# A decoder layer on one core: sums, first evictions, loads and three steps put in another order

## The chip, the cores and the metric

The kernel runs on one core of a Trainium2 chip. The metric is device time in microseconds (us) of one execution; a kernel's time is the median of its runs. Engines: TensorE (PE) multiplies matrices into PSUM; ScalarE (ACT) and VectorE (DVE) read PSUM and SBUF and write SBUF; GpSimd (POOL) does small work on SBUF; SyncE (SP) issues transfers (DMA). Each engine works through its own queue in order, and semaphores hold one engine until another has finished something.

## What is computed

One layer with two token mixers side by side, for 256 tokens of width 1024, all in float32:

```python
n = rms_norm(h, norm1_g)
proj = n @ w_in            # moba q,k,v | gla q,k,v, gate-down, out-gate | branch gates
mq = rms_norm(mq per head); mk = rms_norm(mk per head)          # 8 heads of 64
y_moba = softmax(mq @ mk.T * 64**-0.5 + t5_bias, causal) @ mv
log_a = log_sigmoid(g_low @ gla_gate_up + gla_gate_bias) / 16
y_gla = rms_norm(gla(gq, gk, gv, log_a), gla_out_norm_g) * silu(g_out)   # 4 heads, dk 128, dv 256
mixed = sigmoid(gate_moba) * (y_moba @ w_branch_moba) + sigmoid(gate_gla) * (y_gla @ w_branch_gla)
h = h + mixed @ w_out
h = h + relu(rms_norm(h, norm2_g) @ w_up)**2 @ w_down
```

With 256 tokens there is one MoBA block, so MoBA is plain causal attention with a bias by distance.

## The kernel before

**Precision in halves.** Every float32 operand of a large matmul is used as a high part in float32r and a low part, x - high. Weights come from HBM into `raw` tiles of 128 x 2048 (1 MB, a *unit* of half the depth and 512 columns, numbered 0 to the end); `split` (line 87) has ACT write the high part `wh` (L94, two pieces of 1024), and `rest` (line 97) has DVE write the low part `wl` (L98, two pieces), one slot later through `defer` and `flush`. There are four `raw` tiles; when the second low piece of unit i is written, `rest` issues the load of unit i + 4 on SP (`load`, line 79, L85).

**The projection.** The loop at line 749 runs over 13 column groups (`IN_ORDER`), each of two units, and each unit over two token tiles: a *slot* is one unit and one token tile, slot number 2 * unit + tile. `block` (line 114) multiplies a plain unit, 12 matmuls of 512 columns a slot; `block_t` (line 122) a transposed one (GQ and GK, GLA's q and k), 8 of 512 and 8 of 256. Behind the block a slot runs `flush`, then `split` of the unit two further on, then the eviction of a finished group, and then the steps that `at(slot, ...)` has put there. This order in the text is the order in every engine's queue.

**The start.** Units 0 and 1 (MQ, MoBA's q) come with x in `xw` tiles and are multiplied by `first_block` while they arrive. The evictions of MQ and MK need `rstd`, one over the root mean square of each token: `x_stats` sums the squares of the x tiles `xs` on ACT (L237), DVE and POOL finish it (L218, L219). So MQ and MK are evicted late, at slots 5 to 8: `m_evac` copies (L301) and squares (L303) on ACT, and DVE and POOL make the heads' norms.

**The steps that are touched.** `split_bias`, `make_bias`, `spread_bias` and `load_bias` make the table of biases: a small matmul, a copy u to SBUF, u to DRAM (`ud`, 12 KB), spread there to 128 rows (`ur`, 1.5 MB), and read back skewed into `bias` (1 MB); all three transfers stand in SP's queue. `g_diag` and `g_row` turn `rstd` into a row (matmul `prow`), which GLA's q and k need. `m_norm` and `m_transpose` norm q and k of MoBA and transpose them into `mqH`, `mqL`, `mkH`, `mkL` (high on ACT L287, low on DVE L288). `m_scores0` (line 336, matmuls L334) multiplies the first 128 tokens and DVE scales and adds the bias (L345); `m_max`, `m_softmax`, `m_weights` follow, and `m_scores1` twice for the other tokens. g_evac (line 536) evicts a transposed slot: a copy `half` on ACT (L542) and two instructions on DVE (L545, L546). `m_evac` of MV writes `mvH` on ACT (L287) and `mvL` on DVE (L288).

Of the kernel before, what the change touches and what calls it, by code (L numbers as in the profile page):

```python
# [22 lines left out]
H = 8  # L23
# [12 lines left out]
MQ, MK, MV, GQ, GK, GV0, GV1 = 0, 512, 1024, 1536, 2048, 2560, 3072  # L36
GLOW = 3584
GO0, GO1, GA0, GA1, GG0, GG1 = 3600, 4112, 4624, 5136, 5648, 6160
TRANSPOSED = (GQ, GK)
IN_ORDER = (MQ, MK, GQ, GK, MV, GV0, GV1, GO0, GO1, GA0, GG0, GA1, GG1)  # L40


V_G2, V_GB, V_OG, V_QG, V_KG, NVEC = 0, 8, 12, 14, 15, 16
# [3 lines left out]
def block_kernel(ctx, tc, xw0_d, xw_d, x_d, vec_d, w_d, up_d, bias_d, out_d):  # L47
    nc = tc.nc
    P = 128
# [14 lines left out]
    def mid(name):  # L64
        return t2.tile([P, 512], F32, name=name, tag="t2")
# [4 lines left out]
    def mmbank(name):  # L70
        return ps.tile([P, 512], F32, name=name, tag="mm")

    def axbank(name):
        return ps.tile([P, 512], F32, name=name, tag="ax")
# [4 lines left out]
    def load(i, pieces=1):  # L79
        if i >= NHU:  # L80
            return
        raw[i] = wp.tile([P, 4, 512], F32, name=f"raw{i}", tag="raw", bufs=4)
        n = 4 // pieces
        for a in range(0, 4, n):
            nc.sync.dma_start(raw[i][:, a:a + n, :], w_d[i - 2, :, a:a + n, :])  # L85

    def split(i, a, n=2):
        if i >= NHU:
            return
        if a == 0:  # L90
            wH[i] = wp.tile([P, 4, 512], F32R, name=f"wh{i}", tag="wh")
            wL[i] = wp.tile([P, 4, 512], F32R, name=f"wl{i}", tag="wl")
        s = slice(a, a + n)
        nc.scalar.activation(wH[i][:, s, :], raw[i][:, s, :], AF.Copy)  # L94
        defer(rest, i, s)
# [10 lines left out]
    def defer(f, *a):  # L106
        deferred.append((f, a))

    def flush():
        now, deferred[:] = list(deferred), []  # L110
        for f, a in now:
            f(*a)
# [26 lines left out]
    vec = const.tile([P, NVEC + 128], F32, name="vec")  # L139
# [10 lines left out]
        nc.sync.dma_start(xw[kt], xw_d[kt - 1])  # L150
    load(2, 2)
    load(3)
    nc.sync.dma_start(vec, vec_d)

    NBR = bias_d.shape[0]
    smallR, smallS = big("smallR"), big("smallS", F32R)
# [66 lines left out]
    xs = [big(f"xs{t}") for t in range(NT)]  # L223
    for t in range(NT):
        nc.sync.dma_start(xs[t], x_d[:, t, :])
    nc.sync.dma_start(biasR, bias_d)
    nc.sync.dma_start(gup, up_d)
    load(4)
    load(5)

    rstd = const.tile([P, NT], F32, name="rstd")
# [14 lines left out]
    T = {}  # L246
# [15 lines left out]
    bias = t4.tile([P, H, 256], F32, name="bias", tag="t8", bufs=3)  # L262
# [5 lines left out]
    def make_bias():  # L268
        pb = axbank("pbias")
        nc.tensor.matmul(pb[:H, :384], biasS[:, :H], biasS[:, H:], start=True, stop=True)  # L270
        u = mid("u")[:H, :384]
        nc.vector.tensor_copy(u, pb[:H, :384])
        T["ud"] = dr.tile([H, 384], F32, name="ud")
        nc.sync.dma_start(T["ud"], u)

    def spread_bias():

        T["ur"] = dr.tile([P, H, 384], F32, name="ur")
        nc.sync.dma_start(T["ur"], T["ud"][None].to_broadcast([P, H, 384]))

    def load_bias():
        ur = T["ur"]
        nc.sync.dma_start(bias, bass.AP(tensor=ur.tensor, offset=ur.offset + 127,
                                        ap=[[H * 384 - 1, P], [384, H], [1, 256]]))

    def split_evac(dH, dL, src, scale):
# [5 lines left out]
    def m_evac(which, t, acc):  # L292
        if which == "mv":
            if t == 0:
                T["mvH"], T["mvL"] = (big(f"mv{a}", F32R).rearrange("p (t c) -> p t c", t=2) for a in "HL")
            split_evac(T["mvH"][:, t, :], T["mvL"][:, t, :], acc, rstd[:, t:t + 1])
            return
        if t == 0:
            T[which] = big(which)
        dst = T[which].rearrange("p (t c) -> p t c", t=2)[:, t, :]  # L300
        nc.scalar.activation(dst, acc, AF.Copy, scale=rstd[:, t:t + 1])  # L301
        sq = mid("sq")
        nc.scalar.activation(sq, acc, AF.Square, scale=rstd[:, t:t + 1])  # L303
        r = T[which, "r", t] = small("rsm", H)

        def finish():
            ss = small("ssm", H)
            nc.vector.tensor_reduce(ss, sq.rearrange("p (h d) -> p h d", d=DH), axis=AX.X, op=OP.add)
            rsqrt(r, ss, DH)

        defer(finish)
# [224 lines left out]
    def g_evac(which, h, acc):  # L536

        if h == 0:
            T[which] = big(which)
        v = T[which][:, h * S:(h + 1) * S]  # L540
        half = mid("half")[:, :S]
        nc.scalar.activation(half, acc[:, S:], AF.Copy)  # L542

        def finish():
            nc.vector.tensor_tensor(v, acc[:, :S], half, op=OP.add)  # L545
            nc.vector.scalar_tensor_tensor(v, v, DK ** -0.5 if which == "gq" else 1.0, rrow,  # L546
                                           op0=OP.mult, op1=OP.mult)

        defer(finish)
# [96 lines left out]
    def silu_evac(g, t, acc):  # L646
        if t == 0:
            T["silu", g] = big(f"silu{g}").rearrange("p (t c) -> p t c", t=2)
        sg = mid("sg")
        nc.scalar.activation(sg, acc, AF.Sigmoid, scale=rstd[:, t:t + 1])  # L650
        nc.vector.scalar_tensor_tensor(T["silu", g][:, t, :], acc, rstd[:, t:t + 1], sg,
                                       op0=OP.mult, op1=OP.mult)
# [6 lines left out]
    def gv_evac(g, t, acc):  # L659
        if t == 0:  # L660
            for a in "HL":
                T["gv" + a, g] = big(f"gv{a}{g}", F32R).rearrange("p (t c) -> p t c", t=2)
        split_evac(T["gvH", g][:, t, :], T["gvL", g][:, t, :], acc, rstd[:, t:t + 1])

    evac = {
        MQ: lambda t, a: m_evac("mq", t, a), MK: lambda t, a: m_evac("mk", t, a),
        MV: lambda t, a: m_evac("mv", t, a),
        GQ: lambda t, a: g_evac("gq", t, a), GK: lambda t, a: g_evac("gk", t, a),
        GV0: lambda t, a: gv_evac(0, t, a), GV1: lambda t, a: gv_evac(1, t, a),
        GO0: lambda t, a: silu_evac(0, t, a), GO1: lambda t, a: silu_evac(1, t, a),  # L670
        GA0: lambda t, a: gate_evac("A", 0, t, a), GA1: lambda t, a: gate_evac("A", 1, t, a),
        GG0: lambda t, a: gate_evac("G", 0, t, a), GG1: lambda t, a: gate_evac("G", 1, t, a),
    }


    steps = {}

    def at(slot, f, *a):
        steps.setdefault(slot, []).append((f, a))

    at(5, split_bias)
    at(8, make_bias)
    at(4, x_stats)
    at(6, g_diag)
    at(7, low_split)
    at(8, g_row)
    at(9, gup_split)
    at(9, m_norm, "mq", 0)
    at(10, m_norm, "mq", 1)
    at(10, spread_bias)  # L690
    at(11, m_norm, "mk", 0)
    at(11, g_low)
    at(12, m_norm, "mk", 1)
    at(13, m_transpose, "mq", 0)
    at(13, m_transpose, "mq", 1)
    at(14, g_decay, 0)
    at(14, g_decay, 1)
    at(14, load_bias)
    at(15, m_transpose, "mk", 0)
    at(15, m_transpose, "mk", 1)  # L700
    at(16, m_scores0)
    at(16, m_max, 0)
    at(17, m_softmax, 0, 0, 4)
    at(18, m_softmax, 0, 4, 8)
    at(19, m_scores1, 0)
    at(19, m_max, 1)
    at(19, m_weights, 0)
    at(20, m_softmax, 1, 0, 2)
    at(21, m_softmax, 1, 2, 4)
    at(22, m_scores1, 1)  # L710
    at(22, m_max, 2)
    at(22, m_weights, 1)
    at(23, m_softmax, 2, 0, 2)
    at(24, m_softmax, 2, 2, 4)
    at(25, g_logsig)
    at(26, g_scan)
    at(26, m_weights, 2)
    at(27, g_exp, "eb")
    at(28, g_exp, "einv")
    at(29, g_exp, "edec")  # L720
# [24 lines left out]
    at(50, g_yT, 1, 1)  # L745


    hu = 0
    for u, col in enumerate(IN_ORDER):
        acc = [] if col in TRANSPOSED else [(axbank if u == 1 else mmbank)(f"acc{t}") for t in range(NT)]  # L750
        for g in range(2):
            if u == 0:
                for k in range(4):
                    first_block(4 * g + k, acc)
            for t in range(NT):
                if col in TRANSPOSED:
                    acc = mmbank("acct")
                    for k in range(2):
                        block_t(hu, t, k, xHL[k], acc)
                elif u:  # L760
                    block(hu, t, xH[g], xL[g], acc[t], g == 0, g == 1)
                flush()
                split(hu + 2, 2 * t)
                if g == 1 and u < 2:
                    at(5 + 2 * u + t, evac[col], t, acc[t])
                elif col in TRANSPOSED:
                    evac[col](2 * g + t, acc)
                elif g == 1:
                    evac[col](t, acc[t])
                for f, a in steps.pop(2 * hu + t, []):  # L770
                    f(*a)
            hu += 1
    assert not steps


    mxH = [kview(big(f"mxH{g}", F32R)) for g in range(2)]
# [58 lines left out]
    for n in range(2):  # L835
        acc = [mmbank(f"po{t}") for t in range(NT)]
# [77 lines left out]
    acc = [axbank(f"pu{j}") for j in range(4)]  # L914
# [15 lines left out]
    for c in range(1, NC):  # L930
        for b in range(2):
            for j in range(2):
                acc = axbank(f"pu{j}")
# [86 lines left out]
```

## Time and profile before

| | us |
|---|---|
| median of 3 runs (424.61 to 425.13) | 424.98 |
| the profiled execution | 424.48 |
| its span, first to last instruction | 422.8 |
| PE busy | 412.9 (98%) |
| weight loads into PE busy | 345.5 (82%) |
| DVE busy | 285.9 (68%) |
| ACT busy | 222.5 (53%) |
| mean granted clock of PE | 0.991 |

The profile is of one execution. Busy time of PE counts matmuls whose ends are modelled, so PE is busy nearly all the time and what matters is where it is not, and where its clock is granted at half (the page's line PEclk shows one slice of 40 at 6 tenths, near 63 to 74 us, and 9 or more in all others). The DMA engines are busy 50% of the span on SP's queue, and nearly all of the time from 5 to 30 us.

### The profile page before, as it was taken

The numbers are of one execution on the slowest core, as the hardware profiler recorded it, in microseconds if no ns is written. First come the engines' busy times: TensorE is split into PE (matmuls) and PEld (weight loads), VectorE is DVE, ScalarE is ACT, GpSimd is POOL, SyncE is SP. The second block draws the span as 40 slices with busy tenths as digits, with TensorE's granted clock in tenths as the row PEclk, the third lists the DMA queues.
The fourth block names the chain that finished last, engine by engine and source line by source line (L and its number), as shares of the span: only waits on it lengthen the run. The fifth ranks groups of instructions, "written<-read, shape, count | busy, mean of one in ns | idle before, by whom it ended". The sixth has DMA issues, their size and how long they took to land.

```text
span 422.8 us, 5266 instructions
## 1 busy us (share of the span) xinstructions
PE 412.9 (98%) x2072; PEld 345.5 (82%) x2072; DVE 285.9 (68%) x374; ACT 222.5 (53%) x344; POOL 17.8 (4%) x21
## 2 busy tenths in 40 slices
PE   8999979999999999999999999999999999999996
PEld 5877957888888888888888888888888888888885
DVE  5838987688798543874856878848393848474753
ACT  5669562869865464553423446646362726263520
POOL 2006100000002011000000000000000000000000
PEclk9999996999999999999999999999999999999999
DMA  8995783245544252372675445645455463627002
GB/s 281 381 372 203 258 289 122 87 189 200 198 164 156 86 194 99 135 279 84 219 279 188 136 174 198 228 172 212 186 184 214 147 250 112 287 101 298 0 2 99
DMA packets 13848, 78.91 MB, mean 187 GB/s; under 512 B 1448, under 2 KB 3104, under 8 KB 5376
## 3 DMA queue, kind: packets, MB, share of 16 engines
q1 hardware_dynamic: 13392, 77.28, 50.0%
q10 hardware_dynamic: 432, 1.31, 0.9%
q8 instruction: 16, 0.26, 0.2%
q14 instruction: 8, 0.07, 0.0%
HBM read 77.52 MB, written 2.63 MB: 190 GB/s over the span
## 4 chain that ended last, share of the span: by engine, by line
PE 84%; DMA 5%; DVE 5%; ACT 4%; issue 1%; SPq 0%; ACTq 0%
PE pu L131 14%; PE acc L118 8%; PE acc L119 8%; PE acc L120 8%; PE pu L133 7%; PE fa L119 7%; PE fa L120 7%; PE fa L118 7%; DMA raw<-w 4%; PE po L118 2%; PE po L120 2%; PE pg L118 2%; PE po L119 2%; PE pg L120 2%; PE pg L119 2%; DVE wl L98 2%
## 5 line engine op out<-in xcount | busy, mean ns | idle before, releaser
L98 DVE TENSOR_TENSOR wl<-raw,wh 128x1024 fp32r<-128x1024 f32 x132 | 158.2, 1220 | 18.9 <-ACT wh L94 18.7
L94 ACT ACTIVATE wh<-raw 128x1024 fp32r<-128x1024 f32 x132 | 135.2, 1051 | 24.4 <-PE pg L120 9.8
L131 PE MATMUL pu<-hHL,wh 128*128 128x512 f32 x256 | 69.9, 394 | 0.0
L118 PE MATMUL acc<-wh,xHL 128*128 128x512 f32 x160 | 64.6, 404 | 0.0
L119 PE MATMUL acc<-wl,xHL 128*128 128x512 f32 x160 | 63.0, 394 | 0.0
L120 PE MATMUL acc<-wh,xHL 128*128 128x512 f32 x160 | 62.9, 393 | 0.0
L131 PEld LDWEIGHTS pu<-hHL,wh 128*128 128x128 f32 x256 | 44.3, 189 | 6.3
L120 PE MATMUL fa<-wh,fL 128*128 128x512 f32 x124 | 48.4, 390 | 0.0
L119 PE MATMUL fa<-wl,fH 128*128 128x512 f32 x124 | 48.4, 390 | 0.0
L118 PE MATMUL fa<-wh,fH 128*128 128x512 f32 x124 | 48.3, 389 | 0.0
L133 PEld LDWEIGHTS pu<-hHL,wl 128*128 128x128 f32 x256 | 39.3, 189 | 5.4
L133 PE MATMUL pu<-hHL,wl 128*128 128x256 f32 x256 | 40.7, 281 | 0.0
L870 ACT ACTIVATE half<-pu 128x256 f32<-128x256 f32 x32 | 12.0, 377 | 54.4 <-PE pu L133 54.4
L871 DVE TENSOR_TENSOR sq<-pu,half 128x256 f32<-128x256 f32 x32 | 13.5, 423 | 34.9 <-ACT half L870 34.2
L120 PEld LDWEIGHTS acc<-wh,xHL 128*128 128x128 f32 x160 | 30.4, 190 | 6.7
L118 PEld LDWEIGHTS acc<-wh,xHL 128*128 128x128 f32 x160 | 30.5, 190 | 6.3
L119 PEld LDWEIGHTS acc<-wl,xHL 128*128 128x128 f32 x160 | 30.6, 191 | 5.7
L120 PEld LDWEIGHTS fa<-wh,fL 128*128 128x128 f32 x124 | 23.3, 188 | 4.9
L118 PEld LDWEIGHTS fa<-wh,fH 128*128 128x128 f32 x124 | 23.3, 188 | 4.7
L119 PEld LDWEIGHTS fa<-wl,fH 128*128 128x128 f32 x124 | 23.3, 188 | 4.7
L876 ACT ACTIVATE fH<-sq 128x512 fp32r<-128x512 f32 x16 | 10.1, 632 | 20.6 <-DVE sq L873 20.6
L131 PE MATMUL acct<-xHL,wh 128*128 128x512 f32 x64 | 17.6, 396 | 0.0
(232 smaller groups left out, 533.8 us busy)
## 6 DMA issues: line engine op xcount, KB each, us to landing
raw<-w SPq DMA_DIRECT2D x65, 1024.0 KB, 4.8
xw<-xw SPq DMA_DIRECT2D x7, 384.0 KB, 6.5
ur<-ud SPq DMA_DIRECT2D x1, 1536.0 KB, 9.2
raw<-w SPq DMA_DIRECT2D x2, 512.0 KB, 7.3
xs<-xs SPq DMA_DIRECT2D x2, 512.0 KB, 8.7
bias<-ur SPq DMA_DIRECT2D x1, 1024.0 KB, 7.4
xr<-xs ACTq DMA_DIRECT2D x2, 512.0 KB, 4.8
out<-o SPq DMA_DIRECT2D x3, 256.0 KB, 2.0
```

The lines of the kernel that those rows point to most:

```text
L94: nc.scalar.activation(wH[i][:, s, :], raw[i][:, s, :], AF.Copy)
L98: nc.vector.tensor_tensor(wL[i][:, s, :], raw[i][:, s, :], wH[i][:, s, :].bitcast(F32), op=OP.subtract)
L118: nc.tensor.matmul(acc, aH[:, k, tk], h, start=start and k == 0, stop=False)
L119: nc.tensor.matmul(acc, aH[:, k, tk], low, start=False, stop=False)
L120: nc.tensor.matmul(acc, aL[:, k, tk], h, start=False, stop=stop and k == 3)
L131: nc.tensor.matmul(acc, tile_(wH, k), a[:, k, :], start=g == 0 and k == 0, stop=False)
L133: nc.tensor.matmul(acc[:, :S], tile_(wL, k), a[:, k, :S], start=False, stop=g == 1 and k == 3)
L870: nc.scalar.activation(half, acc[:, S:], AF.Copy)
L871: nc.vector.tensor_tensor(o, acc[:, :S], half, op=OP.add)
L876: nc.scalar.activation(H, v, AF.Copy)
```

## The change

`IN_ORDER` has MV third, so GQ and GK come a place later (and the weights are laid out in that order). `vec` is loaded behind unit 4 and no longer ahead of x; unit 4 is loaded behind x and ahead of `vec`, `biasR` and `gup`. `ud`, `ur` and `bias` are issued by POOL (`nc.gpsimd`) and no longer by SP. `x_stats` stands at slot 3 and no longer 4. The evictions of MQ and MK stand between `flush` and `split` of slots 4, 5 and 7, 8, where they stood behind `split` of slots 5 to 8. `split_bias` goes from slot 5 to 7, `low_split` from 7 to 8, `make_bias` from 8 to 9, `load_bias` from 14 to 12. `m_scores0` and all that follows of MoBA's softmax go one slot back.

```diff
-IN_ORDER = (MQ, MK, GQ, GK, MV, GV0, GV1, GO0, GO1, GA0, GG0, GA1, GG1)
+IN_ORDER = (MQ, MK, MV, GQ, GK, GV0, GV1, GO0, GO1, GA0, GG0, GA1, GG1)
...
     load(3)
-    nc.sync.dma_start(vec, vec_d)
...
         nc.sync.dma_start(xs[t], x_d[:, t, :])
+    load(4)
+    nc.sync.dma_start(vec, vec_d)
     nc.sync.dma_start(biasR, bias_d)
     nc.sync.dma_start(gup, up_d)
-    load(4)
     load(5)
...
-        nc.sync.dma_start(T["ud"], u)
+        nc.gpsimd.dma_start(T["ud"], u)
...
-    at(5, split_bias)
-    at(8, make_bias)
-    at(4, x_stats)
+    at(3, x_stats)
...
-    at(16, m_scores0)
-    at(16, m_max, 0)
+    at(17, m_scores0)
+    at(17, m_max, 0)
...
                 flush()
+                for f, a in early.pop(2 * hu + t, []):
+                    f(*a)
                 split(hu + 2, 2 * t)
                 if g == 1 and u < 2:
-                    at(5 + 2 * u + t, evac[col], t, acc[t])
+                    early.setdefault(4 + 3 * u + t, []).append((evac[col], (t, acc[t])))
```

ACT's queue behind the splits of unit 3, before; in these rows wh_260 is unit 4, wh_312 unit 5, acc_180 and acc_181 the two token tiles of MQ, xs the x tiles:

```order
L94 ACTIVATE wh_260<-raw_172 128x1024
L237 ACTIVATE junk,ssx<-xs_166 128x1024
L237 ACTIVATE junk,ssx<-xs_167 128x1024
L94 ACTIVATE wh_260<-raw_172 128x1024
L265 ACTIVATE smallS<-smallR 112x392
L301 ACTIVATE mq<-acc_180,rstd 128x512
L303 ACTIVATE sq<-acc_180,rstd 128x512
L94 ACTIVATE wh_312<-raw_174 128x1024
L469 ACTIVATE diag<-diagf 128x256
```

and now, where unit 4 is wh_273 and unit 5 wh_319:

```order
L237 ACTIVATE junk,ssx<-xs_165 128x1024
L237 ACTIVATE junk,ssx<-xs_166 128x1024
L301 ACTIVATE mq<-acc_180,rstd 128x512
L303 ACTIVATE sq<-acc_180,rstd 128x512
L94 ACTIVATE wh_273<-raw_169 128x1024
L301 ACTIVATE mq<-acc_181,rstd 128x512
L303 ACTIVATE sq<-acc_181,rstd 128x512
L94 ACTIVATE wh_273<-raw_169 128x1024
L94 ACTIVATE wh_319<-raw_174 128x1024
```

The sums of x stand ahead of all of unit 4's split, and each of MQ's two evictions ahead of a half of it.

DVE's queue around MoBA's first scores, before; wl_599 is unit 9, wl_679 unit 10, gk and gq the evictions of GLA's k and q, s the scaled scores:

```order
L509 TENSOR_SCALAR gm<-pz,vec 128x256 x4
L98 TENSOR_TENSOR wl_599<-raw_374,wh_598 128x1024
L545 TENSOR_TENSOR gk<-acct,half 128x256
L546 SCALAR_TENSOR_TENSOR gk<-gk,rrow 128x256
L98 TENSOR_TENSOR wl_599<-raw_374,wh_598 128x1024
L545 TENSOR_TENSOR gk<-acct,half 128x256
L546 SCALAR_TENSOR_TENSOR gk<-gk,rrow 128x256
L288 SCALAR_TENSOR_TENSOR mkL<-pt,vec,mkH 128x4x128 x2
L345 SCALAR_TENSOR_TENSOR s_681<-ps_682,bias 128x4x128
L345 SCALAR_TENSOR_TENSOR s_681<-ps_683,bias 128x4x128
L370 TENSOR_REDUCE nmax<-s_681 128x8
L98 TENSOR_TENSOR wl_679<-raw_450,wh_678 128x1024 x2
```

and now, where wl_571 is unit 9 and wl_653 unit 10:

```order
L546 SCALAR_TENSOR_TENSOR gq<-gq,rrow 128x256
L98 TENSOR_TENSOR wl_571<-raw_369,wh_570 128x1024
L545 TENSOR_TENSOR gq<-acct,half 128x256
L546 SCALAR_TENSOR_TENSOR gq<-gq,rrow 128x256
L288 SCALAR_TENSOR_TENSOR mkL<-pt,vec,mkH 128x4x128 x2
L98 TENSOR_TENSOR wl_653<-raw_430,wh_652 128x1024
L545 TENSOR_TENSOR gk<-acct,half 128x256
L546 SCALAR_TENSOR_TENSOR gk<-gk,rrow 128x256
L345 SCALAR_TENSOR_TENSOR s_681<-ps_682,bias 128x4x128
L345 SCALAR_TENSOR_TENSOR s_681<-ps_683,bias 128x4x128
L370 TENSOR_REDUCE nmax<-s_681 128x8
L98 TENSOR_TENSOR wl_653<-raw_430,wh_652 128x1024
```

The evictions ahead of `mkL` are those of q and no longer of k (v's two low halves stand further up), a low half of unit 10 and one of k's evictions have come between `mkL` and the scaled scores, and the other half of unit 10 is behind them.

POOL's queue behind the start, before:

```order
L219 TENSOR_TENSOR rstd<-rsv,mhalf 128x2
L219 TENSOR_TENSOR rsm<-rsv,mhalf 128x8 x4
L563 COPY gx<-eb 128x4x64
L568 COPY gx<-edec 128x4x64
L570 MEMSET at_1261 128x1024
```

and now:

```order
L218 TENSOR_TENSOR rstd<-rsv,mhalf 128x2
L218 TENSOR_TENSOR rsm<-rsv,mhalf 128x8 x4
L274 DMA ud<-u 8x384
L279 DMA ur<-ud 128x3072
L283 DMA bias<-ur 128x8x256
L563 COPY gx<-eb 128x4x64
L568 COPY gx<-edec 128x4x64
```

The three transfers stand between the powers and GLA's copies; on SP they are gone from between the loads.

## Rows read from the trace of the kernel before

**Rows 1.** Who PE waited for, from the table of waits: total us, times, longest.

```profile
PE ps L334 <- DVE mkL L288: 2.9, 1, 2.9
...
PE prow L478 <- ACT diag L469: 0.7, 1, 0.7
PE ps L334 <- ACT mkH L287: 0.7, 1, 0.7
PE acct L133 <- DVE wl L98: 0.6, 1, 0.6
```

**Rows 2.** Busy table: start:end, length, busy of five engines, PEclk, DMA share, GB/s.

```profile
20.00:25.00 5.00, 5.00 (x23) 4.14 (x23) 1.00 (x1) 0.00 (x0) 0.00 (x0) 1.00 1.03 353
...
30.00:35.00 5.00, 3.56 (x18) 2.38 (x17) 4.45 (x10) 4.44 (x9) 1.64 (x1) 1.00 0.74 280
...
80.00:422.80 342.80, 339.37 (x1709) 286.63 (x1707) 229.74 (x282) 173.08 (x252) 6.45 (x5) 1.00 0.46 169
...
64.00:65.00 1.00, 0.60 (x6) 0.61 (x8) 1.00 (x2) 0.00 (x0) 0.00 (x0) 0.50 0.75 180
...
70.00:71.00 1.00, 1.00 (x5) 0.83 (x4) 1.00 (x2) 1.00 (x7) 0.00 (x0) 0.77 0.00 0
```

**Rows 3.** PE's timeline, 27 to 75 us: start, us, instruction, count, idle before it.

```profile
27.75 1.07 PE L131 MATMUL acct<-xHL,wh 128*128 128x512 f32 x4
...
33.38 1.09 PE L131 MATMUL acct<-xHL,wh 128*128 128x512 f32 x4
...
41.77 0.27 PE L488 MATMUL plow<-xHL,lowS 128*96 128x256 f32 x1
...
43.65 1.08 PE L131 MATMUL acct<-xHL,wh 128*128 128x512 f32 x4
...
64.39 0.47 PE L334 MATMUL ps<-mkL,mqH 64*128 64x128 f32 x1 [2.92 <-DVE mkL L288]
...
67.15 0.79 PE L118 MATMUL acc<-wh,xHL 128*128 128x512 f32 x1
...
71.53 0.40 PE L118 MATMUL acc<-wh,xHL 128*128 128x512 f32 x1
...
74.26 0.39 PE L118 MATMUL acc<-wh,xHL 128*128 128x512 f32 x1
```

**Rows 4.** ACT's timeline, 25 to 30 us.

```profile
25.06 1.06 ACT L94 ACTIVATE wh<-raw 128x1024 fp32r<-128x1024 f32 x1 [5.50 <-DMA raw<-w]
26.02 1.05 ACT L237 ACTIVATE junk<-xs 128x1024 f32<-128x1024 f32 x1
...
29.48 0.67 ACT L301 ACTIVATE mq<-acc,rstd 128x512 f32<-128x512 f32 x1
```

**Rows 5.** DVE's timeline, 29 to 84 us.

```profile
29.60 0.16 DVE L266 TENSOR_TENSOR smallS<-smallR,smallS 48x8 fp32r<-48x8 f32 x1 [1.20 <-ACT smallS L265]
29.78 1.23 DVE L98 TENSOR_TENSOR wl<-raw,wh 128x1024 fp32r<-128x1024 f32 x1
...
33.02 1.22 DVE L98 TENSOR_TENSOR wl<-raw,wh 128x1024 fp32r<-128x1024 f32 x1
...
52.86 0.42 DVE L545 TENSOR_TENSOR gk<-acct,half 128x256 f32<-128x256 f32 x1
...
63.60 1.40 DVE L288 SCALAR_TENSOR_TENSOR mkL<-pt,vec,mkH 128x512 fp32r<-128x512 f32 x2
67.03 1.29 DVE L345 SCALAR_TENSOR_TENSOR s<-ps,bias 128x512 f32<-128x512 f32 x2 [2.04 <-PE ps L334]
...
69.50 2.35 DVE L98 TENSOR_TENSOR wl<-raw,wh 128x1024 fp32r<-128x1024 f32 x2
...
83.04 0.75 DVE L288 SCALAR_TENSOR_TENSOR mvL<-acc,rstd,mvH 128x512 fp32r<-128x512 f32 x1
```

**Rows 6.** The page's DMA issues: KB each, median us from issue to landing.

```profile
ur<-ud SPq DMA_DIRECT2D x1, 1536.0 KB, 9.2
...
bias<-ur SPq DMA_DIRECT2D x1, 1024.0 KB, 7.4
```

More of the change, by code (lines that the diff above doesn't have):

```diff
@@ L273, in make_bias @@
         T["ud"] = dr.tile([H, 384], F32, name="ud")
-        nc.sync.dma_start(T["ud"], u)
+        nc.gpsimd.dma_start(T["ud"], u)
     def spread_bias():
         T["ur"] = dr.tile([P, H, 384], F32, name="ur")
-        nc.sync.dma_start(T["ur"], T["ud"][None].to_broadcast([P, H, 384]))
+        nc.gpsimd.dma_start(T["ur"], T["ud"][None].to_broadcast([P, H, 384]))
     def load_bias():
         ur = T["ur"]
-        nc.sync.dma_start(bias, bass.AP(tensor=ur.tensor, offset=ur.offset + 127,
+        nc.gpsimd.dma_start(bias, bass.AP(tensor=ur.tensor, offset=ur.offset + 127,
                                         ap=[[H * 384 - 1, P], [384, H], [1, 256]]))
@@ L679, in at @@
         steps.setdefault(slot, []).append((f, a))
-    at(5, split_bias)
-    at(8, make_bias)
-    at(4, x_stats)
+    at(3, x_stats)
     at(6, g_diag)
-    at(7, low_split)
     at(8, g_row)
+    at(7, split_bias)
+    at(8, low_split)
     at(9, gup_split)
+    at(9, make_bias)
     at(9, m_norm, "mq", 0)
@@ L693, in block_kernel @@
     at(12, m_norm, "mk", 1)
+    at(12, load_bias)
     at(13, m_transpose, "mq", 0)
@@ L697, in block_kernel @@
     at(14, g_decay, 1)
-    at(14, load_bias)
     at(15, m_transpose, "mk", 0)
     at(15, m_transpose, "mk", 1)
-    at(16, m_scores0)
-    at(16, m_max, 0)
[L703 to L714, printed above, removed]
+    at(17, m_scores0)
+    at(17, m_max, 0)
+    at(18, m_softmax, 0, 0, 4)
+    at(19, m_softmax, 0, 4, 8)
+    at(20, m_scores1, 0)
+    at(20, m_max, 1)
+    at(20, m_weights, 0)
+    at(21, m_softmax, 1, 0, 2)
+    at(22, m_softmax, 1, 2, 4)
+    at(23, m_scores1, 1)
+    at(23, m_max, 2)
+    at(23, m_weights, 1)
+    at(24, m_softmax, 2, 0, 2)
+    at(25, m_softmax, 2, 2, 4)
     at(25, g_logsig)
     at(26, g_scan)
-    at(26, m_weights, 2)
+    at(27, m_weights, 2)
     at(27, g_exp, "eb")
@@ L745, in block_kernel @@
     at(50, g_yT, 1, 1)
-    hu = 0
+    hu, early = 0, {}
     for u, col in enumerate(IN_ORDER):
@@ L772, in block_kernel @@
             hu += 1
-    assert not steps
+    assert not steps and not early
     mxH = [kview(big(f"mxH{g}", F32R)) for g in range(2)]
```

## The prediction

> **What bounds the kernel now.** I read four views, in this order. First what TensorE (PE) waited for: after the start it has four waits, 2.9, 0.7, 0.7 and 0.6 us [rows 1]. Three belong to the first stretch (weights' low half, the diagonal for `prow`), the largest to the first score matmuls, which stood until the low half of the normed and transposed k (`mkL`) was written. Second, the busy table by stretch [rows 2]: from 80 us on PE is busy 339.37 of 342.80 us at a granted clock of 1.00, so nothing is to be had there; all that the change can win lies before 72 us. The same table shows the clock: it stays 1.00 (2.4 GHz) in 30 to 35 us, where PE was busy only 3.56 of 5, but it is 0.50 (1.2 GHz) from 64 us, after the long wait, until it comes back inside 70 to 71 (0.77).
>
> Third, PE's own timeline [rows 3], to price stalls and slow clock in one number. PE starts unit 4 at 27.75 and has done the scores and both of the next slots' blocks at 71.53: 43.78 us. The undisturbed work in it: a slot of a transposed unit lasts (41.77 - 33.38) / 3 = 2.80, a plain one 74.26 - 71.53 = 2.73, `g_low` 43.65 - 41.77 = 1.88, the 24 score matmuls half of 67.15 - 64.39 = 1.4 at full clock, and the small ones (bias, `prow`, 16 transposes, decay) an estimate of 2.5 from their starts in the same timeline. Eight transposed and two plain slots: 22.4 + 5.5 + 1.9 + 1.4 + 2.5 = 33.7. So PE lost 10.1 us here. The other way of counting, waits of 4.9 plus 0.17 for each of the four (a matmul's row lasts 0.40 but the next starts 0.23 after it, so a wait reads that much short) plus half of the 6 us at half clock, gives 8.6. I take 10.1 as what there is, and 8.6 as the lower end. Fourth, ACT and DVE in front of that wait: both are backed up from 25 to 64 us, after ACT had stood 5.5 us for the weights of unit 4 [rows 4].
>
> **Part 1: x's sums and the evictions of q ahead of the splits, loads reordered.** The x tiles landed long before they were used: unit 4's weights landed at 25.06 [rows 4], and behind x in the queue lay 1.05 MB of these and 0.37 MB of bias and gate tables; at the 353 GB/s of the stretch from 20 us [rows 2] that is 4.0 us, so x was there at about 21.0. Before, the two sums began at 26.02, behind the first split. Now they run in ACT's idle time: the second from 21.0 to 22.2, and by the distance of the sums' end from the first eviction (26.02 + 2 x 1.05 to 29.48, 1.4 us through DVE and POOL) `rstd` is there at 23.5 [rows 4]. With vec, bias and gate tables (0.45 MB) put behind them, unit 4's weights land 1.3 earlier, at 23.8. ACT then does q's first eviction until 24.7 (two of about 0.6), half a split until 25.7, the second eviction until 26.8, the other half until 27.8; DVE ends the second low half at 29.05 (1.23 each [rows 5]). PE wants that piece with the eighth matmul of unit 4, at 27.75 + 7 x 0.2275 = 29.34. So the 0.6 wait goes, with 0.3 to spare. The bound on the bad side: x landing 1 us later costs 0.7. On the good side nothing more is to be won here. The diagonal is then done at about 30.3 and PE reaches `prow` at 30.5: the 0.7 goes too, or leaves up to 0.3.
>
> **Part 2: v third, q and k of GLA a place back, scores a slot back.** PE's work is the same; only its order changes. PE reaches the scores after 4 plain and 6 transposed slots: 27.75 + 10.9 + 16.8 + 1.9 + 2.5 = 59.9. What counts is when DVE has written the first `mkL`, since 0.35 after the first score matmul the second wants it. Before, DVE ran from the first low half of unit 5 at 33.02 to the end of the first `mkL`, 63.60 + 0.74 = 64.34, in 31.3 us with little idle [rows 5]. In the new order four pairs of k's evictions (8 x 0.42 = 3.4) are behind `mkL`, two low halves of v (2 x 0.75 = 1.5) ahead of it, and the bias table's small split (0.16, and up to the 1.2 that DVE waited for ACT there before) also comes into this stretch. Instructions on DVE overlap by some 0.09, so the net is between -2.0 and -0.5; I take -1.1, since the wait for ACT recurs: 30.2 us. The start: before, unit 5's first low half began 2.0 after unit 4's last ended (29.78 + 1.23 to 33.02); a reduction of 0.7 in between is now done earlier, so 1.3: 29.05 + 1.3 = 30.35. So `mkL` is there at 60.55, 0.6 after PE, with bounds of -0.3 and +1.9. The extra slot between transposes and scores (2.80) is what decides it: without it PE would stand there 3.4.
>
> A stall of 0.6 leaves the clock alone by the nearest row (two such stalls in 30 to 35 us, clock 1.00 [rows 2]); one of 2.9 cost it. So with the long wait goes the half clock, worth about 3.
>
> **Part 3: bias by POOL's queue.** The transfers `ud`, `ur`, `bias` leave SP's queue for POOL's. SP saves three issues, and one weight load no longer stands behind `ur`; weight loads were not late after 25 us, so that is worth 0. On POOL only the four powers stand ahead, and nothing behind until GLA's copies late in the kernel. But DVE's first scaled scores need `bias`, and behind them on DVE stands the second low half of unit 10. POOL has u at about 38.8; with 2 to 3 us for the 12 KB, 9.2 for `ur` and 7.4 for `bias` (what they took from SP [rows 6]) it lands at 58 to 59. DVE gets the scores at 61.9. It could begin as late as 65.4: scores and maximum take 69.50 - 67.03 = 2.5, the low half 1.2 [rows 5], and PE wants it two transposed slots and seven matmuls after the scores, at 69.1. So the cover is 6 us: cost 0. That POOL's own issue is slower than SP's no row here shows.
>
> On that one page speaks against the change. The Trainium skill (SBUF — State Buffer, section SBUF: two separate sides) says that a transfer issued from GpSimd has its descriptors written by GpSimd's cores, which VectorE locks out while it runs an operation in a two-port mode; by that rule the three transfers start late when VectorE is as busy as here. No run here shows it yet; the third rival is this, priced from rows.
>
> **Sum.** 10.1 that PE lost, less 0.6 at `mkL`, less 0.2 for what may be left at `prow`: 9.3. Profiled execution 424.48 (span 422.8 and 1.7 around it) - 9.3 = 415.2; the median is 0.5 above the profiled run, so 415.7. After 80 us the other engines have room: DVE is busy 229.74 and ACT 173.08 of 342.80 [rows 2], so an earlier PE doesn't catch up with them; 0 for the rest, at most 1.
>
> **Rivals.**
> 1. *`mkL` is still late.* If x lands a microsecond or two later, or DVE's queue doesn't shrink by 1.1 but by 0, PE stands 2 to 2.5 at the scores and the clock falls again (3): 425.0 - 10.1 + 5.2 = 420. For it: DVE has hardly any idle time in that stretch, every delay on it counts. Against: it takes the bad end of two bounds at once. With the stall alone and the clock kept, 417 to 418. Chance 0.16 for the first, and the second belongs to the forecast's upper flank.
> 2. *It doesn't do what it says:* PE's time just moves on, to the low halves of units 10 to 12, which DVE now reaches behind scores and k's evictions. By my walk unit 10's is written at 65.6 against a need of 69.1, so it would have to slip by over 3; each microsecond more is one lost, at 8 nothing is left: 421 to 424.9. Chance 0.05.
> 3. *Slower: bias is late from POOL.* If POOL's three transfers take twice the rows' time (38 instead of 19), bias lands at 77, DVE stands at the scores with unit 10's low half behind it, PE stalls 12 and the clock falls for 3: 415.7 + 15 = 431. It costs from a landing of 65.4 on, and decides from 71.7 on (6.3 of stall and 3 of clock eat the gain). For it: rows of the trace don't show a single transfer from POOL. Against: that would be 33 us for what took 19. Chance 0.06; a landing between, 0.03.
>
> **How the numbers follow.** The forecast, 414 to 418, has 0.70, rival 1 0.16, rival 2 0.05, rival 3 0.06 (and 0.03). The range goes from 413.9 (the whole 10.1 and 1 more) to 420.2, with rival 1: about 0.82. A measurement of this kernel tells 0.2%, 0.85 us, from no change. Faster by more: the forecast, rival 1, most of rival 2 and the landing between, 0.91; within it 0.03; slower 0.06.
>
> **What would show it.** In the profile after: the two sums on ACT start before 22 and the first eviction of q before 24; PE's waits for `wl` in unit 4 and for `diag` are gone; the wait for `mkL` is under 1.5 and the granted clock stays 1.00 from 5 to 80 us; DVE's first scaled scores wait for PE, not for a DMA; from the scores' end on PE runs as before, some 9 us earlier. It is wrong if the clock shows 0.50 near 60 us, if a weight split waits for a DMA after 30 us, or if PE has a new wait for `wl` of unit 10 or 11.

## The result, and the profile after

The changed kernel takes 414.38 us (median of 4 runs, 414.22 to 414.52); the kernel before, beside it on the same chip, 424.80 (423.94 to 425.13). The ratio is 0.9758 with a 95% interval of 0.9741 to 0.9775: 10.4 us less, where the prediction had 9.3 (415.7, range 413.9 to 420.2).

The page of the profile after: the span, the engines' busy time, PE's granted clock in 40 slices, and two of the DMA issues (KB each, us to landing).

```profile
span 412.8 us, 5269 instructions
...
PE 408.8 (99%) x2072; PEld 343.1 (83%) x2072; DVE 286.0 (69%) x374; ACT 223.0 (54%) x344; POOL 21.5 (5%) x24
...
PEclk9999999999999999999999999999999999999999
...
ur<-ud POOLq DMA_DIRECT2D x1, 1536.0 KB, 9.2
...
bias<-ur POOLq DMA_DIRECT2D x1, 1024.0 KB, 8.3
```

The span is 10.0 shorter than the 422.8 of before. PE's busy time fell by 4.1 only (412.9 to 408.8), although its matmuls are the same: most of that is the halved clock, in which the same matmuls count as longer work. The rest of the 10.0 is waiting. What PE still waited for, with the columns of [rows 1], is one row, of the warm-up at the very start:

```profile
PE pwarm L167 <- PEq L1014: 0.8, 1, 0.8
```

All four waits of [rows 1] are gone, and nothing has come in their place. The busy table by stretch, with the columns of [rows 2]:

```profile
30.00:35.00 5.00, 5.00 (x25) 4.07 (x24) 3.61 (x9) 5.00 (x11) 2.02 (x1) 1.00 0.65 272
60.00:65.00 5.00, 5.00 (x44) 4.46 (x44) 4.93 (x8) 1.70 (x4) 0.00 (x0) 1.00 0.44 180
65.00:70.00 5.00, 5.00 (x27) 4.04 (x25) 4.92 (x8) 5.00 (x20) 0.00 (x0) 1.00 0.60 210
80.00:412.80 332.80, 329.65 (x1663) 278.63 (x1660) 221.92 (x273) 166.89 (x240) 6.50 (x5) 1.00 0.46 169
```

PE is busy 5.00 of 5 us where it was 3.56 (30 to 35), and the clock is 1.00 from 60 to 70, where it showed 0.50 [rows 2]. Behind 80 us PE misses 3.15 of 332.80, as it missed 3.43 of 342.80 before: nothing was won or lost there.

PE's timeline, with the columns of [rows 3]: the start of unit 4, `prow`, the transposes of k, the first two pairs of score matmuls, and the start of unit 10.

```profile
27.64 0.39 PE L118 MATMUL acc<-wh,xHL 128*128 128x512 f32 x1
...
30.37 0.40 PE L478 MATMUL prow<-diag,ones 128*128 128x256 f32 x2
...
53.46 1.03 PE L324 MATMUL pt<-ident,mk 128*128 128x128 f32 x8
...
60.04 0.34 PE L334 MATMUL ps<-mkH,mqH 64*128 64x128 f32 x2
60.20 0.28 PE L334 MATMUL ps<-mkL,mqH 64*128 64x128 f32 x2
...
67.24 0.39 PE L118 MATMUL acc<-wh,xHL 128*128 128x512 f32 x1
```

The matmul that takes `mkL` starts 0.16 behind the first, with no wait. ACT's timeline at the start, which answers to [rows 4]:

```profile
19.27 1.04 ACT L237 ACTIVATE junk<-xs 128x1024 f32<-128x1024 f32 x1
...
20.31 1.04 ACT L237 ACTIVATE junk<-xs 128x1024 f32<-128x1024 f32 x1
...
22.47 0.69 ACT L301 ACTIVATE mq<-acc,rstd 128x512 f32<-128x512 f32 x1 [1.03 <-POOL rstd L218]
...
23.63 1.06 ACT L94 ACTIVATE wh<-raw 128x1024 fp32r<-128x1024 f32 x1
```

The sums run at 19.27 and 20.31, where they ran from 26.02 on; q is evicted from 22.47, where it was 29.48; and the split of unit 4 follows at 23.63 without a wait, where ACT had stood 5.50 us for its weights. DVE's timeline, which answers to [rows 5]:

```profile
26.82 1.23 DVE L98 TENSOR_TENSOR wl<-raw,wh 128x1024 fp32r<-128x1024 f32 x1
...
29.63 1.22 DVE L98 TENSOR_TENSOR wl<-raw,wh 128x1024 fp32r<-128x1024 f32 x1
...
58.88 1.40 DVE L288 SCALAR_TENSOR_TENSOR mkL<-pt,vec,mkH 128x512 fp32r<-128x512 f32 x2
...
62.12 1.28 DVE L345 SCALAR_TENSOR_TENSOR s<-ps,bias 128x512 f32<-128x512 f32 x2
...
64.58 1.22 DVE L98 TENSOR_TENSOR wl<-raw,wh 128x1024 fp32r<-128x1024 f32 x1
```

Unit 4's last low half is done at 28.05 (before, 31.01), the first `mkL` at about 59.6 (half of the pair of 58.88; before, 64.3), and the scaled scores start at 62.12 with nothing in brackets: DVE stood for no transfer. POOL's issues:

```profile
38.74 0.73 POOL L274 DMA_DIRECT2D ud<-u  x1
40.94 0.56 POOL L279 DMA_DIRECT2D ur<-ud  x1 [1.47 <-DMA ud<-u]
50.44 0.92 POOL L283 DMA_DIRECT2D bias<-ur  x1 [8.94 <-DMA ur<-ud]
```

With 8.3 us for it, `bias` landed at 50.44 + 8.3 = 58.7, 3.4 before DVE wanted it.

### The profile page after: what moved, and what is told of

Read it like the earlier page. It is cut to its first block, busy times and chain, and to the rows that moved or that the text cites. A ratio compares the mean times of both kernels' runs of the same rounds, so it can differ in the third digit from the quotient of the medians.

```text
span 412.8 us, 5269 instructions
## 1 busy us (share of the span) xinstructions
PE 408.8 (99%) x2072; PEld 343.1 (83%) x2072; DVE 286.0 (69%) x374; ACT 223.0 (54%) x344; POOL 21.5 (5%) x24
## 3 DMA queue, kind: packets, MB, share of 16 engines
q10 hardware_dynamic: 432, 1.31, 0.9%
## 4 chain that ended last, share of the span: by engine, by line
PE 99%; DVE 0%; issue 0%
PE pu L131 14%; PE acc L118 9%; PE acc L120 9%; PE acc L119 9%; PE pu L133 7%; PE fa L119 7%; PE fa L120 7%; PE fa L118 7%; PE acct L131 4%; PE acct L133 2%; PE po L118 2%; PE po L120 2%; PE po L119 2%; PE pg L119 2%; PE pg L118 2%; PE pg L120 2%
## 5 line engine op out<-in xcount | busy, mean ns | idle before, releaser
L118 PE MATMUL acc<-wh,xHL 128*128 128x512 f32 x160 | 63.6, 398 | 0.0
L120 PE MATMUL acc<-wh,xHL 128*128 128x512 f32 x160 | 62.4, 390 | 0.0
L878 ACT ACTIVATE fH<-sq 128x512 fp32r<-128x512 f32 x16 | 10.1, 632 | 20.6 <-DVE sq L875 20.6
```

What stands on the lines that cost most here:

```text
L118: nc.tensor.matmul(acc, aH[:, k, tk], h, start=start and k == 0, stop=False)
L120: nc.tensor.matmul(acc, aL[:, k, tk], h, start=False, stop=stop and k == 3)
L878: nc.scalar.activation(H, v, AF.Copy)
```

## The experiments

Ten kernels: five with one part of the change taken back ("undo"), three with one part alone put into the kernel before ("only"), two with one transfer made late. Ratios are to the kernel before on the same chip. The runs come from several chips, on which the kernel before has medians of 424.2 to 425.0, so differences below about 1 us between kernels of different chips tell little. The new slots of the steps of the bias table (`split_bias` to `load_bias`) were not taken back by themselves.

**The scores at their old slot** (*undo_slot*): everything but the slot that the scores went back.

```diff
-    at(17, m_scores0)
+    at(16, m_scores0)
-    at(17, m_max, 0)
+    at(16, m_max, 0)
...
-    at(27, m_weights, 2)
+    at(26, m_weights, 2)
```

> The changed kernel with MoBA's scores and softmax steps back at their old slots (16 and on); all else as changed. My theory, that PE's loss at the scores is the time between PE's arrival and the first low half of k: that low half is written at 59.6 us as in the changed kernel, and PE arrives one transposed slot (2.8) earlier, so a stall of 2.3: 414.4 + 2.3 = 416.7 if the granted clock stays at 1.00, and 419.7 if it falls to 0.50 as it did after 3.6 us before. A rival, that the shorter queues of ACT and DVE alone brought the gain and the slot nothing: 414.4, no wait at the scores.

Measured: 419.37 (418.5 to 421.85), ratio 0.9882 (0.9833 to 0.9931). PE's wait at the scores, from its table of waits, and three rows of its busy table, a microsecond each:

```profile
PE ps L334 <- DVE mkL L288: 2.7, 1, 2.7
```

```profile
61.00:62.00 1.00, 0.55 (x6) 0.55 (x6) 1.00 (x2) 0.00 (x0) 0.00 (x0) 0.76 0.78 205
62.00:63.00 1.00, 1.00 (x14) 1.00 (x12) 0.06 (x1) 0.00 (x0) 0.00 (x0) 0.50 1.01 426
...
68.00:69.00 1.00, 1.00 (x7) 0.86 (x7) 0.97 (x3) 0.00 (x0) 0.00 (x0) 0.83 0.00 0
```

The slot's 2.8 us come back as a wait of 2.7, and behind it PE runs at the lower level until inside 68 to 69 (0.50 in all six rows from 62 to 68). The loss in this run is 0.24 + 6 x 0.5 + 0.17 = 3.4 us of full-clock work. By the medians the slot is worth 5 us, less than the wait and the clock of the run shown together: two of the four runs have a mean clock of 0.996 where this one has 0.992, and lost less to it. (The run shown also waited 1.8 us at the start for the first weights, where the other runs of these kernels wait 0 to 1.0, and began unit 4 at 28.3, 0.7 later than the change. Its span of 420.1 is high by that.)

**v back in fifth place** (*undo_v*):

```diff
-IN_ORDER = (MQ, MK, MV, GQ, GK, GV0, GV1, GO0, GO1, GA0, GG0, GA1, GG1)
+IN_ORDER = (MQ, MK, GQ, GK, MV, GV0, GV1, GO0, GO1, GA0, GG0, GA1, GG1)
```

> The changed kernel with MoBA's v back in fifth place (GLA's q and k in third and fourth); all else as changed. My theory: four evictions of k on DVE (3.2 us) come back ahead of the first low half of k, two low halves of v (1.3) go behind it, so it is written 1.9 later, at 61.5, and PE, there at 60.0, stalls 1.5: 415.9 with the clock kept, 418.9 if it falls. A rival, that v's place matters because of the early stretch (a plain unit needs its weights' low half later than a transposed one): a wait for a weights' low half in unit 4, near 30 us, and no wait at the scores; 415 to 415.5.

Measured: 416.14 (415.92 to 419.06), ratio 0.9813 (0.9763 to 0.9862). Two of PE's waits, and a row of the busy table:

```profile
PE ps L334 <- DVE mkL L288: 1.0, 1, 1.0
...
PE pt L324 <- DVE mqL L288: 0.5, 1, 0.5
```

```profile
60.00:65.00 5.00, 4.02 (x34) 3.19 (x33) 4.93 (x9) 1.76 (x2) 0.00 (x0) 1.00 0.60 210
```

v's place is worth 1.5 to 2: without it DVE writes the first `mkL` 2.0 later (from 60.84), PE waits 1.0 and 0.5, and the clock stays at 1.00. One of the four runs, 419.06, has a mean clock of 0.995 where the others have 0.999 to 1.0: there it did fall, though no trace shows where.

**Sums and evictions at their old places** (*undo_sums*; the loads stay as changed):

```diff
-    at(3, x_stats)
+    at(4, x_stats)
...
-                for f, a in early.pop(2 * hu + t, []):
-                    f(*a)
...
-                    early.setdefault(4 + 3 * u + t, []).append((evac[col], (t, acc[t])))
+                    at(5 + 2 * u + t, evac[col], t, acc[t])
```

> The changed kernel with x's sums back at slot 4 and the evictions of MoBA's q and k behind the splits of slots 5 to 8; loads, v, scores and POOL's queue as changed. My theory: ACT does the sums after half a split of unit 4, so the factor of the norms is there at 27.5 instead of 22.4; the early wait for the weights' low half stays away, since the weights land early, the one for prow is 0.1 to 0.5; DVE is 1.5 later at the first low half of k: a stall of 1.1 there: 415.5 to 416. If the sums are worth what the two early waits of before showed: 1.6, no wait at the scores, also 416, so the place of the waits decides. If they are worth nothing: 414.4.

Measured: 415.61 (415.48 to 416.25), ratio 0.9787 (0.9749 to 0.9825), with a wait of 0.2 at the scores and PE busy 4.84 of 5 us from 30 to 35. Worth 1.2. The expected stall of 1.1 at the scores is not there; more was lost at `prow`, whose pair lasted 0.85 and not 0.40 and started 0.24 late behind unit 4's first slot:

```profile
30.54 0.85 PE L478 MATMUL prow<-diag,ones 128*128 128x256 f32 x2
```

Unit 4 itself has no wait in this run, although ACT sums x behind half of its split.

**The old order of loads** (*undo_loads*):

```diff
+    nc.sync.dma_start(vec, vec_d)
...
-    load(4)
-    nc.sync.dma_start(vec, vec_d)
     nc.sync.dma_start(biasR, bias_d)
     nc.sync.dma_start(gup, up_d)
+    load(4)
     load(5)
```

> The changed kernel with the old order of loads: vec ahead of the weights, unit 4's tile behind the bias and gate tables. My theory: the load order alone delays unit 4's landing by 1.3 to 1.7 us; its low halves, done at 28.05 against a need at about 29.3 in the changed kernel, then come just in time or a few tenths late (a wait of 0 to 0.5 us at unit 4), and the high projection of the scores is pushed to a wait of 0 to 0.6 us: 414.4 to 415.2. The rival, that the load order is what removed the early waits: waits of 0.6 and 0.7 us at unit 4 and at the sums come back, 415.7 or more.

Measured: 414.96 (414.3 to 415.58), ratio 0.978 (0.9742 to 0.9818). The table of waits of the profiled run has one wait more than that of the change, 1.0 us at the start for the first weights. PE's timeline also has unit 4's eighth matmul 0.46 behind the seventh, twice the usual 0.23: with the next one 0.3 is lost there, inside the 0 to 0.5 that was expected. The order of loads is worth 0.6 at most, and the intervals don't tell that from nothing. ACT's row of the second sum shows what else the loads do:

```profile
21.48 1.06 ACT L237 ACTIVATE junk<-xs 128x1024 f32<-128x1024 f32 x1 [0.62 <-DMA xs<-xs]
```

Behind `vec`, x itself lands later; in the change this sum began at 20.31 without a wait. So the early waits can't be put down to one of the two parts: with ACT's old order alone 0.7 is lost at `prow` and nothing at unit 4 (*undo_sums*), with the old loads alone 0.3 at unit 4 and nothing at `prow`, and with both old the waits of [rows 1] are there.

**The three transfers back on SP** (*undo_pool*; `ud`, and likewise `ur` and `bias`):

```diff
-        nc.gpsimd.dma_start(T["ud"], u)
+        nc.sync.dma_start(T["ud"], u)
...
```

> The changed kernel with the three transfers of the bias (ud, ur, bias) back on SP's queue. My theory, that this part is worth nothing: 414.4, within 0.3, no new wait of PE; bias lands within 2 us of 58.8. A rival, that the transfers on SP hold up the loads of units 10 and 11 and so the splits: a wait for a load or a weights' half on PE between 45 and 75 us, 415 or more.

Measured: 414.94 (414.25 to 415.25), ratio 0.9771 (0.9726 to 0.9816); no wait but a 0.3 at the start. The median is 0.6 above the change, more than the 0.3 that was expected, but the fastest run is below it: the queue is worth nothing that can be told apart.

**Each part alone, on the kernel before.** First the slot (*only_slot*: the first diff of this section, the other way, on the kernel before):

> The kernel before with the scores and softmax one place back and nothing else changed. My theory: mkL is ready as before (64.3 or so), TensorE comes to the scores one unit of matmuls (2.8 us at full clock) later, so that a wait of 0 to 1.3 us is left at the scores; the clock stays at 1.00 from 60 to 70 and gives back what the halved clock cost; the early waits of 0.6 to 0.7 us stay. Time 418.5 to 420.5. If the clock still falls behind the smaller wait: 421.5 to 423. The rival, that only the earlier operands do it: 424 to 425.

Measured: 418.91 (417.41 to 419.36), ratio 0.9868 (0.9827 to 0.9908). PE's waits but those of the start, and the busy table:

```profile
PE ps L334 <- DVE mkL L288: 1.0, 1, 1.0
...
PE prow L478 <- ACT diag L469: 0.7, 1, 0.7
PE acct L133 <- DVE wl L98: 0.7, 1, 0.7
```

```profile
60.00:65.00 5.00, 4.03 (x22) 3.03 (x23) 4.93 (x9) 4.74 (x7) 0.00 (x0) 1.00 0.65 197
65.00:70.00 5.00, 5.00 (x38) 4.26 (x37) 4.97 (x7) 0.83 (x2) 0.00 (x0) 1.00 0.43 177
```

DVE's work is untouched (the first `mkL` is written from 63.81, as before from 63.60), the early waits are still there, and half of the whole gain is in: 2.6 of waits (2.9 and 0.7 became 1.0) and the clock. Then the sums, the evictions, the new order of loads and the new slots of the bias steps (*only_sums*, in part):

```diff
-    at(4, x_stats)
+    at(3, x_stats)
...
                 flush()
+                for f, a in early.pop(2 * hu + t, []):
+                    f(*a)
                 split(hu + 2, 2 * t)
...
```

> The kernel before with x's sums and the first evictions ahead of the splits and the new load order; v in its old place, scores in their old place, the three bias transfers on SP. My theory: the waits at unit 4 (0.6 and 0.7) go, but TensorE then comes to the scores earlier and waits there for mkL some 3 us, the clock falls as before: 422 to 424. The rival, that early work is what the change is worth: under 418.

Measured: 422.05 (421.02 to 422.69), ratio 0.9943 (0.9922 to 0.9964). PE's waits at the scores, and the busy table:

```profile
PE ps L334 <- DVE mkL L288: 2.9, 1, 2.9
...
PE ps L334 <- ACT mkH L287: 0.7, 1, 0.7
```

```profile
60.00:65.00 5.00, 3.33 (x24) 3.14 (x25) 2.93 (x7) 0.85 (x1) 0.00 (x0) 0.64 0.54 210
```

The early waits are gone, but PE and DVE both come to the scores about 2.7 us earlier, and the wait there is what it was, to the tenth. PE also leaves it 2.7 earlier, and that is the gain (2.2 by the medians, from 424.22 on that chip to 422.05). Last, v third (*only_v*: the diff of *undo_v*, the other way, on the kernel before):

> The kernel before with MoBA's values third and GLA's q and k a place back, and nothing else. My theory: the scores' wait shrinks by the 0.9 us by which v third shortened it on top of the early sums (3.6 without it, 2.7 with it), to about 2; the early waits of 0.6 to 0.7 us stay; if the clock falls as it did behind 2.3 to 2.7 us, 422.5 to 424; if a wait of 2 keeps it, 420 to 421. The rival, that the order of the units by itself frees VectorE for mkL: no wait at the scores, under 419.

Measured: 420.78 (420.41 to 422.14), ratio 0.9907 (0.9879 to 0.9936). PE's waits at the scores and in unit 4, and the busy table:

```profile
PE ps L334 <- DVE mkL L288: 2.1, 1, 2.1
PE acc L119 <- DVE wl L98: 1.4, 1, 1.4
```

```profile
61.00:62.00 1.00, 0.48 (x7) 0.48 (x8) 1.00 (x2) 0.00 (x0) 0.00 (x0) 0.90 0.87 180
...
68.00:69.00 1.00, 1.00 (x6) 0.84 (x5) 1.00 (x2) 0.00 (x0) 0.00 (x0) 0.69 0.00 0
```

The wait is the 2 that was expected and the clock fell (0.50 in the six rows between), but the median is 1.7 below the expected 422.5: the run shown took 422.14 at a mean clock of 0.992, the other three 420.4 to 420.9 at 0.995. By that mean the clock was low for less time in those. The table also has 1.4 for unit 4's low half, where 0.6 to 0.7 was expected. Three matmul records are missing ahead of that wait; by the starts (30.34, and 27.72 + 7 x 0.2275 = 29.31 without a wait) it cost 1.0, as much as before (31.06 and 27.75 + 2.3), though ACT could start on unit 4's weights 0.7 earlier in this run. With v third unit 4 is a plain one, which wants its second low half 1.6 us after its start, where GLA's q wanted it after 2.3. So v third brings that need forward, and the early sums and loads are what meets it.

With these, every combination of the three parts has a time. The queue and the loads are taken as the nothing that they measured, and so are the new slots of the bias steps, which no run shows by themselves; "sums" in the second row has the loads and those slots with it:

```
sums   v   slot     us      wait at the scores / clock there
 -     -    -     424.8      2.9 + 0.7   fell
 x     -    -     422.05     2.9 + 0.7   fell
 -     x    -     420.78     2.1         fell
 -     -    x     418.91     1.0         1.00
 x     x    -     419.37     2.7         fell
 x     -    x     416.14     1.0 + 0.5   1.00
 -     x    x     415.61     0.2         1.00
 x     x    x     414.38     0           1.00
```

The slot is worth most wherever it is added (5.0 to 5.9), because of the three it alone brings the wait down so far that the clock stays in the profiled run. The sums make the wait at the scores longer again when v has shortened it (2.1 to 2.7), since they bring PE there earlier.

**`bias` made late.** The prediction's cover is the time that DVE's scaled scores could start later without PE waiting in unit 10. Two kernels load `ur` more than once on POOL's queue, a redundant transfer, so that `bias` lands later and nothing else changes. One more (*late_bias*):

```diff
         nc.gpsimd.dma_start(T["ur"], T["ud"][None].to_broadcast([P, H, 384]))
+        nc.gpsimd.dma_start(T["ur"], T["ud"][None].to_broadcast([P, H, 384]))
```

> The changed kernel with one redundant transfer: ur's load of 1.5 MB is issued twice on GpSimd's queue, so that bias lands some 9 us later, at about 68 instead of 58.75. The prediction's cover says that VectorE's scaled scores can start as late as 65.4 before unit 10's low half is late for TensorE: at 68, a wait of about 2.5 to 3 us at unit 10, 417 to 417.5, and 419 to 420.5 if the clock falls behind it. The rival, that the landing of bias doesn't matter within 10 us: 414.4.

Measured: 418.87 (415.36 to 421.63), ratio 0.9845 (0.9772 to 0.9918). The runs scatter: 415.36 and 416.95 at a mean clock of 0.999 and 1.0, 420.79 and 421.63 at 0.992 (the ratio is without the last). The profiled one is that of 416.95; DVE's scaled scores and PE's waiting matmul in unit 10, from the timelines:

```profile
67.41 1.29 DVE L346 SCALAR_TENSOR_TENSOR s<-ps,bias 128x512 f32<-128x512 f32 x2 [4.67 <-DMA bias<-ur]
```

```profile
71.14 0.50 PE L119 MATMUL acc<-wl,xHL 128*128 128x512 f32 x1 [1.95 <-DVE wl L98]
```

DVE starts the scores 5.3 later than in the change, PE waits 1.95 with the clock kept, and the matmul behind that wait is the eighth of unit 10, the one named in the prediction. So the cover ends at 67.41 - 1.95 = 65.5. Two more (*later_bias*):

> The changed kernel with two redundant transfers: ur's 1.5 MB is issued three times on GpSimd's queue. With one redundant transfer VectorE began the scaled scores at 67.4 and TensorE waited 1.9 us for unit 10's low half, so the cover ended at 65.5. A third transfer is 9 us more: bias lands at 76 to 77, which is the case of the prediction's third rival. My theory: past 65.5 each microsecond of the landing is one of stall: 11 us at unit 10, then 3 for the halved clock, 427 to 430, slower than before. The rival, that TensorE's order lets some of it be caught up by work behind: 420 to 424.

Measured: 426.51 (425.08 to 429.16), ratio 1.0057 (1.0033 to 1.0081): slower than before. The same two rows, and one of the busy table, in which the clock is at 0.50:

```profile
74.05 1.29 DVE L347 SCALAR_TENSOR_TENSOR s<-ps,bias 128x512 f32<-128x512 f32 x2 [12.35 <-DMA bias<-ur]
```

```profile
77.78 0.80 PE L119 MATMUL acc<-wl,xHL 128*128 128x512 f32 x1 [9.24 <-DVE wl L98]
```

```profile
75.00:80.00 5.00, 2.22 (x5) 1.50 (x5) 4.92 (x7) 3.37 (x13) 0.00 (x0) 0.50 0.27 57
```

`bias` landed at 74 and not 76 to 77, so the expected 11 + 3 becomes 8.6 + 3, or 426. A landing 6.6 later cost 7.3 more of waiting (unit 10 also began 0.65 earlier in this run): past the cover nothing of the wait is caught up.

None of the ten beats the change, in which PE has no wait left behind the start.

## Why the prediction was right, and by how much it was off

**What PE had lost: right, but 0.5 too large.** 10.1 was forecast, by subtracting the undisturbed work from PE's timeline; the count of waits and halved clock gave 8.6. Now PE has no wait and no low clock, and the span is 10.0 shorter. Between the start of unit 4 and that of unit 10 PE takes 67.24 - 27.64 = 39.6 us; by the prediction's sizes, four plain and eight transposed slots and the small work are 10.9 + 22.4 + 1.9 + 1.4 + 2.5 = 39.1. So the prediction put the undisturbed work 0.5 too low, and the loss in that stretch was 9.6 and not 10.1; that the span shrank by 10.0 is those 9.6, 0.1 at the start of unit 4 and 0.3 behind 80 us. Of the microsecond by which the count of waits falls short, PE's timeline before shows most:

```profile
32.69 0.85 PE L478 MATMUL prow<-diag,ones 128*128 128x256 f32 x2 [0.72 <-ACT diag L469]
...
56.38 1.31 PE L324 MATMUL pt<-ident,mk 128*128 128x128 f32 x8
```

Behind its listed wait the pair of `prow` lasted 0.85, now 0.40, and the transposes of k 1.31, now 1.03: 0.7 that stands in no row of waits. In its reading of [rows 1] the prediction put three of the four waits into the first stretch; two belong there, and the 0.7 for `mkH` stood at the scores. The sum is the same.

**Part 1: the mechanism right, the size too small.** This is the term that was off. I had x's second tile at 21.0 and the second sum from 21.0 on; it began at 20.31. `rstd` was there at 22.44 and not 23.5, and DVE's last low half of unit 4 was done at 28.05 and not 29.05, 1.2 before PE wanted it and not 0.3. I had worked x's landing back from that of unit 4 in the old order of loads, and there it was about right: in *undo_loads* the second sum stood for x until 21.48. But the new order brings x itself earlier too, since `vec` no longer stands ahead of it. SP's timeline, before and then after, shows x issued 0.6 earlier:

```profile
11.13 0.90 SPq L225 DMA_DIRECT2D xs<-xs  x2
```

```profile
10.53 0.91 SPq L224 DMA_DIRECT2D xs<-xs  x2
```

`prow` at 30.37 had no wait (I kept 0.2). By *undo_loads* the order of loads, to which the prediction gave the 1.3 of unit 4, is worth 0.6 or nothing to the whole, and by *undo_sums* ACT's order is worth 1.2: either alone takes away most of the wait at unit 4, and ACT's order that at `prow`.

**Part 2: right, but for what came from part 1.** PE came to the scores at 60.04 (forecast 59.9); `mkL` was there at 59.6 (forecast 60.55). Unit 5's first low half began at 29.63 on DVE and not at 30.35, which is 0.7 of that; the stretch behind it took 30.0 and not 30.2. So the stall was 0 and not 0.6, inside the bounds of -0.3 to +1.9. With 0.2 at `prow` the gain was put 0.8 too small there; the loss put 0.5 too large made up for part of it, which is luck. The rest of the 1.1 is the 0.1 and 0.3 outside the stretch and 0.4 by which the medians differ more than the profiled runs. What decides it was named rightly: "without it PE would stand there 3.4" and the clock falls; *undo_slot* measured 2.7 and the fall. That the extra slot alone brings half of the gain (*only_slot*) the prediction didn't say; it gave the credit to three edits together.

**The clock: right.** It was put at "about 3". Before, PE worked at half clock from 64.39 until inside 70 to 71 [rows 2, 3], which is 3.0; in *undo_slot* and in *only_v* it was 3.4, by the one-microsecond rows.

**Part 3: right.** Landing 58 to 59 forecast, 58.7 measured; scores on DVE 61.9 forecast, 62.12 measured; unit 10's low half 65.6 forecast, 65.8 measured; the cover's end at 65.4 forecast, 65.5 in *late_bias*. The one page of the Trainium skill that spoke against it (SBUF — State Buffer, section SBUF: two separate sides) would have the descriptors of POOL's transfers held up while DVE is in a two-port mode. Its effect is not in these runs: `ur` took 9.2 from POOL's queue and `bias` 8.3, while DVE was busy 15.92 of the 17.70 us from 41 to 58.7; before, from SP's, they took 9.2 and 7.4 [rows 6], and in *undo_pool* 10.3 and 6.9. Over all twelve kernels `ur` took 8.8 to 10.4 from POOL and 8.9 to 10.3 from SP, `bias` 6.0 to 8.3 and 6.0 to 8.4. The prediction had the transfers start late because DVE is busy; the rule asks for the mode, and whether DVE's operations here take it at all no run shows.

**The rivals.** Rival 1 (`mkL` late by 2 to 2.5, 420) has its price confirmed by *undo_slot*, where PE is early instead: 419.4. Rival 2 (the waits move on to units 10 to 12) did not come: no row of PE's waits names `wl`. Rival 3 was put to the test with *later_bias*: it said that a landing at 77 costs 12 of stall and 3 of clock, and that it decides from 71.7 on. At 74 the stall was 9.2, the time 12.1 above the change, and 1.7 above before. So its price holds within 1 us, and so does its turning point by reckoning: at a microsecond for each, 74.05 - 1.75 = 72.3. Only its cause, a slow queue, wasn't there.

## What to carry to other kernels

Where a wait of some microseconds also costs the clock, look first for a step that can be put one place later in the waiting engine's order: here one slot, 2.8 us of other matmuls ahead of the scores, was worth 5 to 6, as much as both parts that get the operand earlier together (424.8 to 419.37). Making the front of the queue earlier alone moves the wait (*only_sums*: 2.9 before, 2.9 after), since both sides of it come earlier (it still brought the 2.2 of the early waits). Price a hidden transfer by the last start that still hides it: that number came from two timelines, and a profiled run with the transfer made late confirmed it.

## What the runs showed of the hardware that was not expected

PE's granted clock stayed at 1.00 behind waits of 1.0 (*undo_v*, *only_slot*) and 1.9 us (*late_bias*), and fell to the lower level (0.50, 1.2 GHz) behind 2.1 (*only_v*), 2.7 (*undo_slot*), 2.9 (*only_sums*, before) and 9.2 (*later_bias*) in the profiled runs; ahead of the 2.9 stood another wait of 0.7, with one score matmul between. The same kernel doesn't always fall: *late_bias* has runs at a mean clock of 0.999 to 1.0 and of 0.992, 4 to 6 us apart, and *undo_v* one at 0.995 among three at 0.999 to 1.0. Nor, by the mean clock, is the fall always of one length: the ten runs of *only_sums* are 421.02 and 421.04 at 0.995, and 421.7 to 422.7 at 0.988 to 0.992. This is also part of what scatters the kernel before (422.1 to 426.3 in 13 runs, clock 0.987 to 0.995), but not all of it: its runs at 0.991 to 0.992 alone go from 422.4 to 425.6. The changed kernel, at 0.999 to 1.0 in its four runs, stays within 0.3 us.
